# The order of a unit's half products in a hybrid decoder layer: the third factor's two halves around the seventh's

## The chip, the cores and the metric

The kernel runs on one core of one Trainium2 chip. The metric is the device time of one execution in microseconds. Three runs of the kernel before the change took 914.4, 915.17 and 915.88 us; the median is 915.17.

The core has a matrix engine (TensorE, PE in the profile, with the loading of its weights shown apart as PEld), a vector engine (VectorE, DVE), a scalar engine for activations and copies (ScalarE, ACT), a general engine (GpSimd, POOL) and SyncE (SP), which issues DMAs here. Matmuls write to PSUM, a memory of banks, from which ACT or DVE has to fetch the result before a bank can be used again.

## What is computed

The reference is one inference step of one decoder layer over 1024 prompt tokens and 8 decode tokens. All inputs to the branches come from one large projection of the normalised input; then a recurrent branch (RG-LRU) and a matrix memory (mLSTM, four heads of 256, chunks of 128 tokens) run, and a projection leads back:

```python
hn = rmsnorm(x, g_norm)
u = hn @ w_in                                  # 1024 x 1024 @ 1024 x 7176
xa, za, uq, uk, uv, uo, zb, ui, uf = jnp.split(u, SPLIT_IDX, axis=-1)
yA, hA, bufA = rglru_branch(xa, ...)           # conv, gates, linear scan
hB, C, n, m = mlstm_seq(q, k, v, ig, lf, C0, n0, m0)
yB = rmsnorm over a head of (sigmoid(uo) * hB), times g_mhead
merged = jnp.concatenate([yA * silu(za), yB * silu(zb)], axis=-1)
x = x + merged @ w_out
```

The first projection, `hn @ w_in`, is the part that the change concerns.

## The kernel before

Every matrix product is made exact to about float32 from a rounded high part and a low remainder of each operand: `mm3` (lines 64 to 68) issues high x high, high x low and low x high, always as three matmuls, and `split` (lines 70 to 74) makes the two parts with one ACT cast (line 72) and one DVE subtraction (line 73). In the profile nearly all matmuls therefore stand at L66, L67 and L68, and nearly all casts and subtractions at L72 and L73.

**Units and products.** The columns of `w_in` are worked off in 14 units of two blocks of 256 columns each (`UNITS`, line 44; the letters name what a block yields, v, x, y, q, k, o or z). Unit 0 is done while the input is read. A unit is a 2 x 2 block product by the scheme of Strassen and Winograd, with seven products instead of eight: P1, P2, P5, P6, P7, P3, P4 in this order (line 41). The input's seven combinations stand ready in `cb`; the weights' combinations are made unit by unit in `prep` (line 276), which also splits them into `wh` and `wl`. `prep` of P7 and P4 issues the loads of the next unit's weights on SP.

**Half products.** Each product is done in two halves, s = 0 and 1, here called pieces: 12 matmuls of 512 columns (24 of 256 in units of v and o). `product` (line 299) issues both one after the other. Each half has two PSUM accumulators, X (tag `kv`, two banks) and Y (tag `o`, three banks). P1, P6, P7 and P4 add up in the same X; P2 has a Y of its own, and P5 and P3 share the next one. After each piece `evac` (line 325) reads the partial sum:

- P1: ACT copies X to `s1` (L328). P2: DVE adds Y to `s1` (L331), output.
- P5: ACT copies Y to `s5` (L335).
- P6: ACT copies X to `s2` (L338).
- P7: DVE adds X to `s5` (L341), output.
- P3: DVE adds Y to `s2` (L345), output.
- P4: ACT copies X (L353), or applies tanh, output.

Outputs go to memory by `stq`, a DMA on POOL's queue (`emit_out`, line 362); for y and z a SiLU comes first (ACT L359, DVE L360). So P7 of a half must not start before the copy after P6 of that half has ended, and P4 not before the add after P7.

**Buffers.** `wh` and `wl` come from a pool of six (`NWS`), so three products are held; `LEAD = 2` calls `prep` two products ahead, and the split of a product can only begin when the product three before it has been used up. The staging tiles (`s1`, `s2`, `s5` and so on) come from a pool of seven.

**What runs beside it.** After each piece, `pop_bg` (line 711) issues one step, or two in the first and last units, of the background work: gates, the RG-LRU branch, the decode part, the first chunks of the mLSTM. In the last unit, `wo_due(q)` (line 1642), called after product q, appends steps that prepare the output projection: `w_step` splits blocks of `w_out` into buffers that held `cb` (those of P7 for one split, those of P3 for the next two), and `r_op` splits operands from a ring that SP fills, into tiles of the pool of six. After the units, `r_prod` multiplies the ring's operands, interleaved with the mLSTM's chunks.

The program is traced in this order; a scheduler then sorts each engine's instructions, by readiness in a model of the time and by the order of the program among those that are ready. Each engine then runs its list in order.

Of the kernel before, what the change touches and what calls it, by code (L numbers as in the profile page):

```python
# [17 lines left out]
P = 128  # L18
# [4 lines left out]
NH = 4  # L23
# [17 lines left out]
Q_P1, Q_P2, Q_P5, Q_P6, Q_P7, Q_P3, Q_P4 = range(7)  # L41
# [3 lines left out]
NWS, NSTG, LEAD = 6, 7, 2  # L45
# [6 lines left out]
def hymba_kernel(  # L52
# [11 lines left out]
    def mm3(out, ah, al, bh, bl, first, last):  # L64

        TE.matmul(out, ah, bh, start=first, stop=False, skip_group_check=True)  # L66
        TE.matmul(out, ah, bl, start=False, stop=False, skip_group_check=True)  # L67
        TE.matmul(out, al, bh, start=False, stop=last, skip_group_check=True)  # L68
# [13 lines left out]
    def ps(tag, shape):  # L82
        return psp.tile(shape, F32, tag=tag, name=f"ps_{tag}", bufs=NBUF.get(tag, 1))
# [17 lines left out]
    def sg(shape, name, dt=F32):  # L101

        return stg.tile(shape, dt, tag="stg", name=name)
# [116 lines left out]
    late = []  # L220
    lastt = []

    def run_late():
        now = late[:]
        late.clear()
        for f in now:
            f()
# [3 lines left out]
    units = [((c[0], int(c[1])), (c[2], int(c[3]))) for c in UNITS]  # L231
# [39 lines left out]
    wops = {}  # L271
# [24 lines left out]

    px = {}

    def product(u, q):

        kind = units[u][0][0]
        wh, wl = wops.pop((u, q))
        bh, bl = cb[q]
        first, last = q in (Q_P1, Q_P2, Q_P5), q in (Q_P2, Q_P3, Q_P4)
        for s in range(2):
            if q == Q_P1:
                px["X", s] = ps("kv", [P, 512])
            if q in (Q_P2, Q_P5):
                px["Y", s] = ps("o", [P, 512])
            X, Y = px["X", s], px.get(("Y", s))  # L310
            out = X if q in (Q_P1, Q_P6, Q_P7, Q_P4) else Y
            if kind in "vo":
                for i in range(2):
                    t = slice((2 * s + i) * P, (2 * s + i + 1) * P)
                    for k in range(4):
                        mm3(out[:, i * 256:(i + 1) * 256], bh[:, k, t], bl[:, k, t], wh[:, k, :], wl[:, k, :],
                            first and i == 0 and k == 0, last and i == 1 and k == 3)
            else:
                c = slice(s * P, (s + 1) * P)
                for k in range(4):  # L320
                    mm3(out, wh[:, k, c], wl[:, k, c], bh[:, k, :], bl[:, k, :], first and k == 0, last and k == 3)
            evac(u, q, s, X, Y)
            yield

    def evac(u, q, s, X, Y):
        if q == Q_P1:
            px["s1", s] = t = sg([P, 512], "s1")
            A.copy(t, X)  # L328
        elif q == Q_P2:
            t = px.pop(("s1", s))  # L330
            V.tensor_tensor(t, t, Y, op=ALU.add)  # L331
            emit_out(u, 0, 0, s, t)
        elif q == Q_P5:
            px["s5", s] = t = sg([P, 512], "s5")
            A.copy(t, Y)  # L335
        elif q == Q_P6:
            px["s2", s] = t = sg([P, 512], "s2")
            A.copy(t, X)  # L338
        elif q == Q_P7:
            t = px.pop(("s5", s))  # L340
            V.tensor_tensor(t, t, X, op=ALU.add)  # L341
            emit_out(u, 1, 1, s, t)
        elif q == Q_P3:
            t = px.pop(("s2", s))
            V.tensor_tensor(t, t, Y, op=ALU.add)  # L345
            emit_out(u, 0, 1, s, t)
        else:
            t = sg([P, 512], "c21")
            o = units[u][1][0] == "o"
            if o:  # L350
                A.activation(t, X, AF.Tanh, scale=0.5)
            else:
                A.copy(t, X)  # L353
            emit_out(u, 1, 0, s, t, o)
# [170 lines left out]
    kind, j = units[0][0]  # L525
# [183 lines left out]
    bg, rgq, dcq = deque(), deque(), deque()  # L709

    def pop_bg(n=1, rg=1, dc=1):
        run_late()
        for q, m in ((bg, n), (rgq, rg), (dcq, dc)):
            for _ in range(m):
                if q:
                    q.popleft()()
# [38 lines left out]
    def rg_unit(jj):  # L755

        rst["stored"] |= {2 * jj, 2 * jj + 1}
        for j in (2 * jj, 2 * jj + 1):
            for b in range(2):
                n = 2 * j + b  # L760
                h = rg_half(j, b)
                if n % 4 == 0:
                    rgq.append(lambda n=n: rg_load(n, True))
                rgq.extend(h[:-1])
                rgq.append((lambda j=j, f=h[-1]: (f(), rg_dec(j))) if b == 1 else h[-1])
        if jj == 3:
            rgq.extend([rg_final, lambda: None, rg_rows])
# [578 lines left out]
    def w_slot(a, b, n):  # L1346
        w_fetch(a, b, slot(n, f"wc{a}{b}", F32))
# [294 lines left out]
    def wo_due(q):  # L1642

        step = lambda *ns: bg.extend([lambda n=n: w_step(n) for n in ns])
        if q == 0:
            w_slot(0, 0, 0)
            w_slot(1, 0, 1)
        elif q == 1:
            w_slot(1, 1, 2)
        elif q == 2:  # L1650
            bg.append(lambda: dec_block(0))
            step("s3", Q_P1)
        elif q == 3:
# [12 lines left out]
    seq = [(u, q) for u in range(1, len(units)) for q in range(7)]  # L1666
    state = {"prep": 0, "m": False}

    def preps(n):
        while state["prep"] < min(n, len(seq)):  # L1670
            prep(*seq[state["prep"]])
            state["prep"] += 1
# [3 lines left out]
    last_u = len(units) - 1  # L1676
    unit_of = {p: u for u, pair in enumerate(units) for p in pair}
    done_h = [max(unit_of[k, h] for k in "qkv") for h in range(NH)]

    def m_start():  # L1680
        state["m"] = True
        bg.append(m_open1)
        for n in range(NH):
            bg.extend(m_first(n))

    preps(LEAD)
    part = 0
    for n, (u, q) in enumerate(seq):
        preps(n + 1 + LEAD)
        for _ in product(u, q):  # L1690
            pop_bg(2 if u == 1 or u == last_u else 1, 1, part % DEC[1 if u >= DEC[0] else 2] == 1)
            part += 1
        if u == last_u:
            wo_due(q)
        if q == 6:
            for kind, j in units[u]:
                if kind == "x":
                    rg_unit(j)
            for half in range(2):
                if u == max(unit_of["v", 2 * half], unit_of["v", 2 * half + 1], 1):  # L1700
                    bg.append(lambda half=half: dec_rows(half))
            for h in range(NH):
                if done_h[h] == u:
                    bg.append(lambda h=h: dcq.extend(decode_steps(h)))
            if u == last_u - 1:
                dgen = decode_outputs()

                def step():
                    next(dgen, None)
                    run_late()  # L1710
                state["out"] = [step] * 5 + [m_open2]
        if not state["m"] and u > max(done_h) and not (bg or rgq or dcq or late):
            m_start()
        if u == last_u and q == 0:
            if not state["m"]:
                while bg or rgq or dcq or late:
                    pop_bg()
                m_start()
            bg.extend(state["out"])
    while bg or late:  # L1720
        pop_bg()
    with tc.issue_after(lastt[0].ins):
# [6 lines left out]
    last = NCH - 1  # L1729
    N2 = 18  # L1730
    for n in range(4, N):
        c, h = n // 4, n % 4
# [92 lines left out]
```

## Time and profile before

| What | Value |
|---|---|
| Time of the runs | 914.4, 915.17, 915.88 us |
| The profiled execution | 913.23 us, its span 911.3 us |
| Units 1 to 13 on PE | from 72 us to 656 us |
| Busy between 0 and 72 us: PE, DVE, ACT | 68.5, 52.7, 46.3 us |
| Busy between 656 and 911.3 us: PE, DVE, ACT | 247.8, 209.3, 160.3 us |
| Moved by DMA | 167.76 MB, mean 184 GB/s |

A row of the profile names the engine, the line of the kernel, the operation, the tiles (written <- read) and either a duration or a count with the sum and the mean. A bracket at the end of a row gives the idle time of the engine before it and what ended that. Busy time counts an engine's own work, not its waiting for semaphores. The ends of matmuls are modelled, so the row of a matmul says more by its start than by its end.

### The profile page before, as it was taken

The page shows a single profiled execution, that of the slowest core. Times are in us where ns is not written, and L with a number is a line of the kernel's source. Part 1 is how long each engine was busy: PE and PEld are TensorE (multiplying, and loading weights), DVE is VectorE, ACT ScalarE, POOL GpSimd, SP SyncE. Part 2 cuts the span into 40 slices and gives each one's busy share as a digit, 9 for nine tenths or more (in the row PEclk, how much of TensorE's full clock was granted, in tenths as well). Part 3 has the DMA queues.
Part 4 walks back from the last instruction along what each step waited for, and adds up shares of the span by engine and source line. Part 5 has one row for each costly group of instructions (what it writes and reads, how often), then busy time and mean ns, then how long its engine had stood idle before and what let it go on. Part 6 is the DMA issues. An engine that isn't in the chain of part 4 may idle for free. (4 is left out here: it accounts for less than half of the span.)

```text
span 911.3 us, 16738 instructions
## 1 busy us (share of the span) xinstructions
PE 899.6 (99%) x5889; PEld 762.3 (84%) x5889; DVE 739.3 (81%) x1528; ACT 585.0 (64%) x1086; POOL 194.2 (21%) x322
## 2 busy tenths in 40 slices
PE   8999999999999999999999999999999999999996
PEld 6997778877788997887789999887788888888886
DVE  6974778979698978789889876679998879888973
ACT  7653446867567776576658775446786568566642
POOL 1111112122222232324332334010111111121120
PEclk9999999999999999999999999999999999999999
DMA  6412447465746566548665747345679888855531
GB/s 200 149 64 92 139 147 250 135 205 187 236 128 221 171 203 204 197 145 266 201 237 184 253 139 244 108 133 191 215 234 259 202 216 296 217 142 180 181 124 67
DMA packets 130493, 167.76 MB, mean 184 GB/s; under 512 B 17596, under 2 KB 98564, under 8 KB 130402
## 3 DMA queue, kind: packets, MB, share of 16 engines
q1 hardware_dynamic: 108790, 103.68, 37.4%
q0 software_dynamic: 21616, 63.02, 20.9%
q8 instruction: 46, 0.75, 0.3%
q14 instruction: 37, 0.30, 0.1%
q10 hardware_dynamic: 4, 0.00, 0.0%
HBM read 108.00 MB, written 62.92 MB: 188 GB/s over the span
## 5 line engine op out<-in xcount | busy, mean ns | idle before, releaser
L72 ACT CAST wh<-raw 128x1024 fp32r<-128x1024 f32 x91 | 95.4, 1049 | 79.5 <-DVE raw L280 21.0
L73 DVE TENSOR_TENSOR wl<-raw,wh 128x1024 fp32r<-128x1024 f32 x91 | 111.1, 1221 | 29.4 <-ACT wh L72 15.8
L66 PE MATMUL ps_kv<-cb_hi,wh 128*128 128x512 f32 x320 | 127.4, 398 | 0.0
L68 PE MATMUL ps_kv<-cb_hi,wl 128*128 128x512 f32 x320 | 125.5, 392 | 0.0
L67 PE MATMUL ps_kv<-cb_lo,wh 128*128 128x512 f32 x320 | 125.2, 391 | 0.0
L66 PE MATMUL ps_o<-cb_hi,wh 128*128 128x512 f32 x240 | 95.2, 397 | 0.0
L68 PE MATMUL ps_o<-cb_hi,wl 128*128 128x512 f32 x240 | 93.7, 391 | 0.0
L67 PE MATMUL ps_o<-cb_lo,wh 128*128 128x512 f32 x240 | 93.6, 390 | 0.0
L66 PEld LDWEIGHTS ps_kv<-cb_hi,wh 128*128 128x128 f32 x320 | 60.1, 188 | 15.9 <-issue 3.1
L68 PEld LDWEIGHTS ps_kv<-cb_hi,wl 128*128 128x128 f32 x320 | 60.1, 188 | 13.4 <-issue 0.6
L67 PEld LDWEIGHTS ps_kv<-cb_lo,wh 128*128 128x128 f32 x320 | 60.1, 188 | 12.7 <-issue 0.8
L66 PE MATMUL ps_kv<-wh,cb_hi 128*128 128x256 f32 x192 | 55.1, 287 | 0.0
L67 PE MATMUL ps_kv<-wl,cb_hi 128*128 128x256 f32 x192 | 54.4, 283 | 0.0
L68 PE MATMUL ps_kv<-wh,cb_lo 128*128 128x256 f32 x192 | 54.3, 283 | 0.0
L66 PEld LDWEIGHTS ps_o<-cb_hi,wh 128*128 128x128 f32 x240 | 45.1, 188 | 10.4 <-issue 0.8
L68 PEld LDWEIGHTS ps_o<-cb_hi,wl 128*128 128x128 f32 x240 | 45.0, 188 | 9.9
L66 PE MATMUL ps_o<-wo,mh 128*128 128x512 f32 (+1 forms) x136 | 53.0, 390 | 0.0
L67 PEld LDWEIGHTS ps_o<-cb_lo,wh 128*128 128x128 f32 x240 | 45.1, 188 | 8.9
L68 PE MATMUL ps_o<-wo,ml 128*128 128x512 f32 (+1 forms) x136 | 51.6, 380 | 0.0
L67 PE MATMUL ps_o<-wo,mh 128*128 128x512 f32 (+1 forms) x136 | 51.5, 379 | 0.0
L66 PE MATMUL ps_o<-wh,cb_hi 128*128 128x256 f32 x144 | 41.0, 284 | 0.0
L67 PE MATMUL ps_o<-wl,cb_hi 128*128 128x256 f32 x144 | 40.7, 283 | 0.0
(559 smaller groups left out, 2603.8 us busy)
## 6 DMA issues: line engine op xcount, KB each, us to landing
raw<-in_w_in_dram SPq DMA_DIRECT2D x55, 512.0 KB
Cb<-in_state_mlstm_C_dram SPq DMA_DIRECT2D x32, 256.0 KB
out_dram<-Cb POOLq DMA_DIRECT2D x32, 256.0 KB, 4.9
qk<-d_qk SPq DMA_DIRECT2D x32, 256.0 KB
ring<-d_ro SPq DMA_DIRECT2D x26, 256.0 KB
d_qk<-s POOLq DMA_DIRECT2D x24, 256.0 KB, 4.8
d_x<-s POOLq DMA_DIRECT2D x16, 256.0 KB, 2.8
zsr<-d_y SPq DMA_DIRECT2D x16, 256.0 KB
```

What stands on the lines that cost most here:

```text
L66: TE.matmul(out, ah, bh, start=first, stop=False, skip_group_check=True)
L67: TE.matmul(out, ah, bl, start=False, stop=False, skip_group_check=True)
L68: TE.matmul(out, al, bh, start=False, stop=last, skip_group_check=True)
L72: a = A.copy(hi, src)
L73: V.tensor_tensor(lo, src, hi.bitcast(F32), op=ALU.subtract)
```

## The change

`product` is no longer a generator of two halves but issues one half, given as `s`; the weights' tiles are dropped after the second half. The main loop goes over a list of 14 pieces. The first eight are as before. Then come P3's first half, P7's two halves, P3's second half, and P4's two. `PREP` gives the pieces before which `preps` is called: the sixth call, which starts the next unit's P1, comes before piece 11 instead of 10. `DUE` gives the pieces after which `wo_due` is called in the last unit: the call for index 4 comes after piece 10 (before: 9), that for 5 after piece 12 (before: 11).

```diff
-    def product(u, q):
+    def product(u, q, s):
 
         kind = units[u][0][0]
-        wh, wl = wops.pop((u, q))
+        wh, wl = wops.pop((u, q)) if s == 1 else wops[u, q]
...
-        for s in range(2):
...
-            evac(u, q, s, X, Y)
-            yield
...
+        evac(u, q, s, X, Y)
...
+    PIECES = [(q, s) for q in (Q_P1, Q_P2, Q_P5, Q_P6) for s in range(2)]
+    PIECES += [(Q_P3, 0), (Q_P7, 0), (Q_P7, 1), (Q_P3, 1), (Q_P4, 0), (Q_P4, 1)]
+    PREP = 0, 2, 4, 6, 8, 11, 12
+    DUE = 1, 3, 5, 7, 10, 12, 13
+
     preps(LEAD)
     part = 0
-    for n, (u, q) in enumerate(seq):
-        preps(n + 1 + LEAD)
-        for _ in product(u, q):
+    for u in range(1, len(units)):
+        for n, (q, s) in enumerate(PIECES):
+            if n in PREP:
+                preps(7 * (u - 1) + PREP.index(n) + 1 + LEAD)
+            product(u, q, s)
             pop_bg(2 if u == 1 or u == last_u else 1, 1, part % DEC[1 if u >= DEC[0] else 2] == 1)
             part += 1
-        if u == last_u:
-            wo_due(q)
...
+            if u == last_u and n in DUE:
+                wo_due(DUE.index(n))
```

The rest of the loop's body (the steps after a unit, the start of the mLSTM, the output steps of the decode part) is only indented and keyed to the piece's number; it comes after the same count of pieces as before.

More of the change, by code (lines that the diff above doesn't have):

```diff
@@ L297, in hymba_kernel @@
     px = {}
-    def product(u, q):
+    def product(u, q, s):
         kind = units[u][0][0]
-        wh, wl = wops.pop((u, q))
+        wh, wl = wops.pop((u, q)) if s == 1 else wops[u, q]
         bh, bl = cb[q]
         first, last = q in (Q_P1, Q_P2, Q_P5), q in (Q_P2, Q_P3, Q_P4)
-        for s in range(2):
[L306 to L319, printed above, removed]
-                for k in range(4):
-                    mm3(out, wh[:, k, c], wl[:, k, c], bh[:, k, :], bl[:, k, :], first and k == 0, last and k == 3)
-            evac(u, q, s, X, Y)
-            yield
+        if q == Q_P1:
+            px["X", s] = ps("kv", [P, 512])
+        if q in (Q_P2, Q_P5):
+            px["Y", s] = ps("o", [P, 512])
+        X, Y = px["X", s], px.get(("Y", s))
+        out = X if q in (Q_P1, Q_P6, Q_P7, Q_P4) else Y
+        if kind in "vo":
+            for i in range(2):
+                t = slice((2 * s + i) * P, (2 * s + i + 1) * P)
+                for k in range(4):
+                    mm3(out[:, i * 256:(i + 1) * 256], bh[:, k, t], bl[:, k, t], wh[:, k, :], wl[:, k, :],
+                        first and i == 0 and k == 0, last and i == 1 and k == 3)
+        else:
+            c = slice(s * P, (s + 1) * P)
+            for k in range(4):
+                mm3(out, wh[:, k, c], wl[:, k, c], bh[:, k, :], bl[:, k, :], first and k == 0, last and k == 3)
+        evac(u, q, s, X, Y)
     def evac(u, q, s, X, Y):
@@ L1691, in hymba_kernel @@
             pop_bg(2 if u == 1 or u == last_u else 1, 1, part % DEC[1 if u >= DEC[0] else 2] == 1)
             part += 1
-        if u == last_u:
-            wo_due(q)
[L1695 to L1717, printed above, removed]
-                m_start()
-            bg.extend(state["out"])
+            if u == last_u and n in DUE:
+                wo_due(DUE.index(n))
+            if n == 13:
+                for kind, j in units[u]:
+                    if kind == "x":
+                        rg_unit(j)
+                for half in range(2):
+                    if u == max(unit_of["v", 2 * half], unit_of["v", 2 * half + 1], 1):
+                        bg.append(lambda half=half: dec_rows(half))
+                for h in range(NH):
+                    if done_h[h] == u:
+                        bg.append(lambda h=h: dcq.extend(decode_steps(h)))
+                if u == last_u - 1:
+                    dgen = decode_outputs()
+                    def step():
+                        next(dgen, None)
+                        run_late()
+                    state["out"] = [step] * 5 + [m_open2]
@@ L1720, in hymba_kernel @@
+            if n % 2 and not state["m"] and u > max(done_h) and not (bg or rgq or dcq or late):
+                m_start()
+            if u == last_u and n == 1:
+                if not state["m"]:
+                    while bg or rgq or dcq or late:
+                        pop_bg()
+                    m_start()
+                bg.extend(state["out"])
     while bg or late:
```

## The prediction

> **What bounds the kernel now.** I read the head of the page first, then the busy time of each engine in six stretches, then what the matmul engine waited for.
>
> ```profile
> span 911.3 us, 16738 instructions
> PE 899.6 (99%) x5889; PEld 762.3 (84%) x5889; DVE 739.3 (81%) x1528; ACT 585.0 (64%) x1086; POOL 194.2 (21%) x322
> ...
> 72.00:292.00 220.00, 219.59 (x1324) 174.86 (x1321) 173.22 (x324) 136.38 (x201) 43.54 (x78) 1.00 0.54 174
> 292.00:470.00 178.00, 178.00 (x1229) 150.16 (x1221) 150.97 (x253) 120.64 (x172) 52.15 (x82) 1.00 0.62 202
> 470.00:611.00 141.00, 141.00 (x1168) 129.66 (x1168) 110.15 (x201) 91.07 (x148) 42.61 (x64) 1.00 0.57 186
> 611.00:656.00 45.00, 44.65 (x231) 33.54 (x220) 42.96 (x81) 30.26 (x45) 5.62 (x11) 1.00 0.58 194
> ...
> PE ps_s L1069 <- DVE dworkb L1067: 0.4, 1, 0.4
> PE ps_tr L257 <- DMA raw<-in_w_in_dram: 0.3, 1, 0.3
> ```
>
> The four stretches are those of the units whose pieces the change reorders (the columns are the stretch, its length, PE, PEld, DVE, ACT and POOL, the clock, the DMA share and GB/s). PE is busy for 219.59 + 178.00 + 141.00 + 44.65 = 583.24 of 584 us. So 0.76 us is idle, and the last two rows, the waits between 72 and 656 us, say for what: a small vector operation of the decode part and a weight load from memory. No evacuation of a half product is among them. The granted clock (the 1.00 behind the engines) is full. DVE is second, and only in the last 45 us is it nearly as full (42.96).
>
> A busy PE can hide stalls, since the ends of matmuls are modelled. So I look at starts, and at the load of weights beside them.
>
> ```profile
> 406.33 0.39 PE L68 MATMUL ps_kv<-cb_hi,wl 128*128 128x512 f32 x1
> 406.56 0.39 PE L66 MATMUL ps_kv<-cb_hi,wh 128*128 128x512 f32 x1
> ...
> L66 PEld LDWEIGHTS ps_kv<-cb_hi,wh 128*128 128x128 f32 x320 | 60.1, 188 | 15.9 <-issue 3.1 <-ACT xh L813 0.4 <-ACT c L353 0.2
> ```
>
> Start to start is 0.23 us, and the row at 406.56 is the first matmul of P7's first half, right behind P6: the border of two pieces costs no more than any other step. A piece of twelve such matmuls is 2.7 us. The Trainium skill, in "Perfetto Trace Analysis", section "Identifying the Most-Contended Engine", calls matmul busy time a poor measure of headroom and the busy share of weight loads a good one; by it the 84% of PEld would leave a sixth of the time open. Here the trace speaks against that reading: a load of 188 ns in every step of 230 ns is 82%, with the matmuls back to back.
>
> **The change part by part.** No instruction is added or removed, so all that can move the time is a wait, new or gone. Times are those of the profiled execution, 913.23 us (span 911.3 and 1.9 around it); the median of the three runs is 915.17, and I add my sum to the median.
>
> *P3's first half between P6 and P7.* P7 adds to the bank that P6's copy (L338) reads. Today one piece lies between a P6 half and the P7 half on the same bank; after, two. The tightest case of the 26 is unit 8, second half:
>
> ```profile
> 408.19 0.59 ACT L338 COPY s<-ps_kv 128x512 f32<-128x512 f32 x1
> ...
> 409.28 0.39 PE L66 MATMUL ps_kv<-cb_hi,wh 128*128 128x512 f32 x1
> ```
>
> The copy ends at 408.78 and P7 begins at 409.28: 0.5 us to spare without the change. So the wait that the change makes roomier is not there, and this part gains 0.
>
> *P7 closer to P4.* P4 writes the same bank as P7, after the vector engine's add (L341). Three pieces lie between today, two after. The latest add:
>
> ```profile
> 147.92 0.39 PE L68 MATMUL ps_kv<-cb_hi,wl 128*128 128x512 f32 x1
> ...
> 151.67 0.68 DVE L341 TENSOR_TENSOR s<-s,ps_kv 128x512 f32<-128x512 f32 x1
> ```
>
> P7's last matmul began at 147.92 and the next piece at 148.15; the add ended at 152.35, 4.2 us later. Two pieces give 5.4 us. So 1.2 us is left in the worst case: 0.
>
> *P3 needed two pieces sooner.* P3's weights are cast and split while P6 runs, at the same place as before, but are now used right after P6 and not four half products later. The split ends with the vector operation at L73. P3 would begin where P7's first half begins now:
>
> ```profile
> 98.00 1.22 DVE L73 TENSOR_TENSOR wl<-raw,wh 128x1024 fp32r<-128x1024 f32 x1 [4.20 <-PE ps_kv L67]
> 98.06 0.69 PE L616 MATMUL ps_s<-idF,par 49*128 49x49 f32 x8
> 98.69 0.50 PE L66 MATMUL ps_kv<-cb_hi,wh 128*128 128x512 f32 x1
> ...
> 139.83 1.23 DVE L73 TENSOR_TENSOR wl<-raw,wh 128x1024 fp32r<-128x1024 f32 x1
> 142.66 0.39 PE L66 MATMUL ps_kv<-cb_hi,wh 128*128 128x512 f32 x1
> ...
> 315.86 1.22 DVE L73 TENSOR_TENSOR wl<-raw,wh 128x1024 fp32r<-128x1024 f32 x1
> 317.70 0.28 PE L66 MATMUL ps_kv<-wh,cb_hi 128*128 128x256 f32 x1
> ...
> 447.52 1.23 DVE L73 TENSOR_TENSOR wl<-raw,wh 128x1024 fp32r<-128x1024 f32 x1
> 450.00 0.39 PE L66 MATMUL ps_kv<-cb_hi,wh 128*128 128x512 f32 x1
> ...
> 631.65 1.20 DVE L73 TENSOR_TENSOR wl<-raw,wh 128x1024 fp32r<-128x1024 f32 x1
> 637.86 0.39 PE L66 MATMUL ps_kv<-cb_hi,wh 128*128 128x512 f32 x1
> ```
>
> Split's end against P7's start: 99.22 against 98.69 in unit 1 (late by 0.5), then 141.06 / 142.66 (1.6 to spare, unit 2), 317.08 / 317.70 (0.6, unit 6), 448.75 / 450.00 (1.2, unit 9), and 632.85 / 637.86 (5.0, unit 13, the roomiest); the other eight lie between 1.6 and 5.0. In unit 1 the first two matmuls of a triple need only the high part, so two steps of 0.23 us pass first: 0.5 - 0.46 is a stall of 0.1 us. The row at 98.00 also says why it is late: it got its buffer only when P6's last reader was done. Bounds: 0 (other matmuls fill it, as the transposes at 98.06 do now) to 1.3 us (nothing does, so the whole split shows). I take 0.1. Nothing queues behind the wait but the next pieces.
>
> *The next unit's P1 is split one piece later*, since its buffer is P7's. Tightest case, unit 3: the split begun at 152.26 against P1's first matmul.
>
> ```profile
> 152.26 1.22 DVE L73 TENSOR_TENSOR wl<-raw,wh 128x1024 fp32r<-128x1024 f32 x1
> ...
> 161.00 0.50 PE L66 MATMUL ps_kv<-cb_hi,wh 128*128 128x512 f32 x1
> ```
>
> From 153.48 to 161.00 there are 7.5 us; 2.7 less leaves 4.8: 0. P3's and P7's stores on POOL change places, with POOL 21% busy and their staging buffers freed by completion; no SP load moves but those of the tail.
>
> *The last unit's background steps.* Those that follow P7 and P3 (weight splits, ring loads) come one piece later in the program, and P7's buffers come free one piece later.
>
> ```profile
> 645.38 0.62 ACT L72 CAST ro<-ring 128x512 fp32r<-128x512 f32 x1 [1.12 <-PE ps_kv L67]
> ...
> 653.62 0.69 DVE L73 TENSOR_TENSOR ro<-ring,ro 128x512 fp32r<-128x512 f32 x1
> ...
> 656.30 0.39 PE L66 MATMUL ps_o<-wr0h,ro 128*128 128x512 f32 x1
> ```
>
> The cast of the first ring operand waited for a buffer of P7. A piece later it ends at 648.7, still 4.9 us ahead of the vector operation that completes it, so that one need not move. It ends at 654.3, 2.0 us ahead of its matmul. Bounds: 0, and 0.7 us at this matmul if the vector operation slips by a whole piece as well. DVE has the same work and takes P3's add early for P7's late one: I take 0.
>
> Sum: 0.1 us, 915.3.
>
> **Rivals.** *The tail slips by a whole piece (slower).* DVE is full there, and this chain follows:
>
> ```profile
> 667.55 2.28 DVE wr5l L73 x2
> ...
> 670.22 3.89 DMA ring<-d_ro
> ...
> 674.65 0.48 ACT hh L1247
> 675.18 0.66 PE ps_qp L1298 x4
> ```
>
> From the split of the last weights over a ring load to a PE that already waits, each microsecond that DVE loses arrives in full. If DVE idles for the piece that the splits wait, that is 2.7 us: 917.9. It decides once DVE's loss passes 1.8 us. For it: the chain has no slack. Against it: DVE's work is sorted by readiness there, and the ring cast above shows 4.9 us of room. *P3's splits run late in many units (slower).* If the later P1 split of one unit pushes the vector work of the next by d, stalls are 0.1 + d in unit 1 and d less the margins 0.6, 1.2 and 1.6. At d = 2 us that is 2.1 + 1.4 + 0.8 + 0.4 = 4.7: 919.9. It passes 0.2% at about d = 1.2. Against it: in each unit all vector work up to P6 is as before.
>
> *Hidden stalls go (faster).* All idle time of the units, 0.76, and the slow matmuls:
>
> ```profile
> L66 PE MATMUL ps_kv<-cb_hi,wh x320: 387/389/504, 72.5 to 655.6; 128*128 128x512 f32 x160
> ...
> L66 PE MATMUL ps_kv<-cb_hi,wh 128*128 128x512 f32 x320 | 127.4, 398 | 0.0
> L68 PE MATMUL ps_kv<-cb_hi,wl 128*128 128x512 f32 x320 | 125.5, 392 | 0.0
> L67 PE MATMUL ps_kv<-cb_lo,wh 128*128 128x512 f32 x320 | 125.2, 391 | 0.0
> ```
>
> Means of 398, 392 and 391 over a median of 389 ns are 14 ns x 320 = 4.5 us in the four products on this bank, 1.1 for P7's share. With 0.76 that is 1.9: 913.3. It needs every one of them to hang on P6's copy, and the 0.5 us above speaks against. The rule of the Trainium skill on weight loads, taken at its word, would be this case. *The change doesn't do what it says:* where P3's split is late, P7 may still be issued first, since the schedule already interleaves by readiness in the tail. Then the order is partly the old one: 915.2.
>
> **How the numbers follow.** Two runs can be told apart from about 0.2%, or 1.8 us. Forecast, 0.76: 915.3. Order partly unchanged, 0.04: 915.2. Together 0.80 within 0.2%. Tail, 0.07: 917.9, and late splits, 0.06: 919.9; slower 0.13. Hidden stalls, 0.07: 913.3; faster 0.07. The range leaves out these three, 0.20 in all: from 913.6, the lowest run of before (914.4) less all idle time of the units (0.76), to 917.2, the highest run (915.88) and the upper bound of P3's stall in unit 1 (1.3).
>
> **What would show it.** Right: PE idle between 72 and 656 us stays under 1.5 us, the ACT copy L338 ends some 3 us ahead of P7, and unit 1 shows P3's third matmul up to 0.5 us late. Wrong: PE waits on DVE L73 at the start of P3 in units 6, 9 or 2 (late splits); the wait at L1298 near 675 us grows past 2 us, or a new one stands at the first ring matmul (tail); or the spacing at P7 falls and the span with it (hidden stalls).

## The result and the profile after

The changed kernel took 920.4 us (median of six runs, 919.19 to 922.85) against 915.67 us (914.4 to 915.88, six runs) of the kernel before: ratio 1.0051, 95% interval 1.004 to 1.0061. It is slower by half a per cent. The forecast was 915.3 us, with a range from 913.6 to 917.2 us.

The profiled execution took 920.19 us. First the head of its page:

```profile
span 918.4 us, 16730 instructions
PE 901.3 (98%) x5889; PEld 763.0 (83%) x5889; DVE 739.7 (81%) x1528; ACT 585.1 (64%) x1086; POOL 194.6 (21%) x322
```

The counts of PE, DVE, ACT and POOL are those of before, and so are the busy times of DVE, ACT and POOL, within 0.4 us. The work is the same. What grew is mostly waiting; PE's busy time is 1.7 us longer with the same count. The same four stretches as in the prediction (stretch, length, PE, PEld, DVE, ACT, POOL, clock, DMA share, GB/s):

```profile
72.00:292.00 220.00, 218.98 (x1293) 174.09 (x1290) 172.51 (x325) 135.34 (x201) 43.64 (x78) 1.00 0.54 173
292.00:470.00 178.00, 177.64 (x1201) 149.57 (x1204) 146.78 (x244) 118.89 (x170) 51.01 (x79) 1.00 0.61 200
470.00:611.00 141.00, 136.78 (x1145) 125.67 (x1146) 111.00 (x200) 90.49 (x146) 42.80 (x64) 1.00 0.56 183
611.00:656.00 45.00, 44.65 (x276) 33.77 (x275) 41.32 (x84) 26.65 (x41) 5.64 (x11) 1.00 0.55 184
```

PE idles 1.02 + 0.36 + 4.22 + 0.35 = 5.95 us, where before it idled 0.76 us: 5.2 us of the 7.1 us by which the span grew (918.4 against 911.3). The two medians lie only 4.7 us apart, since the profiled execution of before was 2.4 us under its median. The other 1.9 us are not idle time of PE in the units, and nothing here explains them. Most of the idle time, 4.2 us, lies in the third stretch, where before PE had none. What PE waited for between 72 and 656 us (total, times, longest):

```profile
PE ps_kv L66 <- ACT c L351: 2.7, 2, 1.9
PE ps_s L924 <- DVE OC L911: 0.9, 1, 0.9
PE ps_o L66 <- DVE s L329: 0.8, 2, 0.5
PE ps_s L818 <- DVE xh L812: 0.4, 1, 0.4
PE ps_s L1067 <- DVE dworkb L1065: 0.4, 1, 0.4
PE ps_s L655 <- DVE gx L625: 0.3, 1, 0.3
PE ps_kv L66 <- ACT c L349: 0.3, 1, 0.3
```

The lines behind `evac`'s beginning stand two lower than before: L351 is L353 of before, the copy after P4; L329 is L331, the add after P2. The largest wait is a first matmul of P1 in unit 10, which may not write its bank before ACT has copied unit 9's P4 from it. The prediction never looked at that hand-off.

The timeline of **before** around it, first ACT, then DVE and PE:

```profile
456.62 1.05 ACT L72 CAST wh<-raw 128x1024 fp32r<-128x1024 f32 x1 [1.10 <-PE ps_kv L67]
...
462.08 0.72 ACT L988 ACTIVATE Cb<-Cb,dGI 128x512 f32<-128x512 f32 x1 [2.16 <-DMA Cb<-in_state_mlstm_C_dram]
462.71 0.80 ACT L834 ACTIVATE rg<-rg,sp4n 128x512 f32<-128x512 f32 x1
...
467.13 0.59 ACT L353 COPY c<-ps_kv 128x512 f32<-128x512 f32 x1
470.80 0.62 ACT L813 CAST xh<-xc 64x512 fp32r<-64x512 f32 x1 [3.08 <-DVE na L847]
471.84 0.62 ACT L813 CAST xl<-xc 64x512 fp32r<-64x512 f32 x1 [0.42 <-DVE rm L865]
472.48 0.59 ACT L353 COPY c<-ps_kv 128x512 f32<-128x512 f32 x1
...
469.55 1.22 DVE L847 TENSOR_TENSOR_SCAN na<-rg,ig 128x512 f32<-128x512 f32 x1
...
467.80 0.39 PE L68 MATMUL ps_kv<-cb_hi,wl 128*128 128x512 f32 x1
...
473.61 0.39 PE L66 MATMUL ps_kv<-wh,cb_hi 128*128 128x256 f32 x1
```

And **after**:

```profile
466.09 0.72 ACT L986 ACTIVATE Cb<-Cb,dGI 128x512 f32<-128x512 f32 x1 [4.76 <-DMA Cb<-in_state_mlstm_C_dram]
466.72 0.80 ACT L832 ACTIVATE rg<-rg,sp4n 128x512 f32<-128x512 f32 x1
467.43 1.04 ACT L72 CAST wh<-raw 128x1024 fp32r<-128x1024 f32 x1
...
471.99 0.59 ACT L351 COPY c<-ps_kv 128x512 f32<-128x512 f32 x1
475.88 0.62 ACT L811 CAST xh<-xc 64x512 fp32r<-64x512 f32 x1 [3.31 <-DVE na L845]
476.92 0.61 ACT L811 CAST xl<-xc 64x512 fp32r<-64x512 f32 x1 [0.42 <-DVE rm L863]
477.56 0.59 ACT L351 COPY c<-ps_kv 128x512 f32<-128x512 f32 x1
...
462.50 0.68 DVE L339 TENSOR_TENSOR s<-s,ps_kv 128x512 f32<-128x512 f32 x1
...
468.50 1.23 DVE L73 TENSOR_TENSOR wl<-raw,wh 128x1024 fp32r<-128x1024 f32 x1 [0.25 <-ACT wh L72]
...
474.63 1.22 DVE L845 TENSOR_TENSOR_SCAN na<-rg,ig 128x512 f32<-128x512 f32 x1
...
472.63 0.38 PE L66 MATMUL ps_kv<-wh,cb_hi 128*128 128x256 f32 x1 [0.77 <-ACT c L351]
...
478.20 0.38 PE L66 MATMUL ps_kv<-wh,cb_hi 128*128 128x256 f32 x1 [1.90 <-ACT c L351]
```

Read them as one chain through two queues. A load of decode state (`Cb`) ends; ACT, which has stood still for it, scales it (L988, after: L986), then computes an exponential for the RG-LRU branch (L834 / L832). Several vector operations further on, DVE does the branch's scan (L847 / L845). The next casts of that branch on ACT (L813 / L811) write into tiles that the scan and the product behind it (L865 / L863) still read, so they wait for both. Only behind them comes the second copy of P4, though P4 had long ended: in before its last matmul began at 467.80, 4.7 us ahead of that copy. Before, that copy ended at 473.07 and P1's second half began at 473.61: **0.54 us to spare**.

The cast of the next unit's P1 is the row that changed its place. Before, it ran at 456.62, released by one of P7's last matmuls and ahead of the whole chain. After, P7 ends a piece later, DVE's add on it starts at 462.50, and by then ACT already stands at the scale. The cast (467.43) and its subtraction (468.50, 1.23 us on DVE) now run between the exponential and the scan. The Trainium skill, in "Perfetto Trace Analysis", section "Tensor Engine Instruction (MATMUL, LD_WEIGHTS)", says that the queues of ACT and DVE are strictly first in, first out; the 4.76 us that ACT idles with that cast behind the scale agree.

So two things make the copy late. From the scale to the second copy it took 472.48 - 462.08 = 10.40 us before and 477.56 - 466.09 = 11.47 us after: 1.07 us more. And the scale itself began 4.01 us later. The rest of this text asks which part of the change is behind that, and whether it is the whole loss.

### The profile page after: what moved, and what is told of

Same layout as the page of the kernel before. It is cut to its first block, busy times and chain, and to the rows that moved or that the text cites. A ratio compares the mean times of both kernels' runs of the same rounds, so it can differ in the third digit from the quotient of the medians.

```text
span 918.4 us, 16730 instructions
## 1 busy us (share of the span) xinstructions
PE 901.3 (98%) x5889; PEld 763.0 (83%) x5889; DVE 739.7 (81%) x1528; ACT 585.1 (64%) x1086; POOL 194.6 (21%) x322
## 5 line engine op out<-in xcount | busy, mean ns | idle before, releaser
L73 DVE TENSOR_TENSOR wl<-raw,wh 128x1024 fp32r<-128x1024 f32 x91 | 110.9, 1219 | 34.3 <-ACT wh L72 19.2
L67 PE MATMUL ps_kv<-cb_lo,wh 128*128 128x512 f32 x320 | 125.2, 391 | 0.0
L67 PE MATMUL ps_o<-cb_lo,wh 128*128 128x512 f32 x240 | 93.6, 390 | 0.0
L67 PEld LDWEIGHTS ps_kv<-cb_lo,wh 128*128 128x128 f32 x320 | 60.1, 188 | 12.7 <-issue 0.8
L67 PE MATMUL ps_kv<-wl,cb_hi 128*128 128x256 f32 x192 | 54.4, 283 | 0.0
L67 PEld LDWEIGHTS ps_o<-cb_lo,wh 128*128 128x128 f32 x240 | 45.1, 188 | 8.8
L67 PE MATMUL ps_o<-wo,mh 128*128 128x512 f32 (+1 forms) x136 | 51.5, 379 | 0.0
L67 PE MATMUL ps_o<-wl,cb_hi 128*128 128x256 f32 x144 | 40.7, 283 | 0.0
```

The source lines that it names most:

```text
L73: V.tensor_tensor(lo, src, hi.bitcast(F32), op=ALU.subtract)
```

## The experiments

Each time is a median, and each ratio is to the kernel before in the same series of runs. There the kernel before had medians of 914.41, 914.1, 914.59 and 914.2 us.

### First series: what the traces suggested

Three ideas were open: the later split of the next unit's P1, P3 between P6 and P7, and the steps of the last unit. A fourth kernel moved the scale.

**The split alone, in the old order.** Only the call that issues the next unit's P1 split comes one piece later:

```diff
-        preps(n + 1 + LEAD)
+        if q != Q_P3:
+            preps(n + 1 + LEAD)
         for s, _ in enumerate(product(u, q)):
...
+            if q == Q_P3 and s == 0:
+                preps(n + 1 + LEAD)
```

> The order of pieces of the kernel before, with one thing of the change: the split of the next unit's P1 is issued one piece later (before P3's second half instead of its first). Theory A (the later split of the next unit's P1 shifts the scalar engine's queue, and P4's copies behind it come too late for the next unit's P1): 919 to 922 us, over 3 us of PE idle between 72 and 656 us, most of it at the start of unit 10 behind the copy L353. Theory B (P3 between P6 and P7 does it: its weights are needed two pieces sooner, and the adds change places): 915 to 916.5 us, under 1.2 us idle there. Theory C (the last unit's steps come later): 915 to 916.5 us as well.

Measured: 913.84 us, ratio 0.9997 (0.9987 to 1.0007). By the time alone the split would be cleared. The timeline of ACT in this run says why it must not be:

```profile
456.29 1.05 ACT L72 CAST wh<-raw 128x1024 fp32r<-128x1024 f32 x1 [1.10 <-PE ps_kv L67]
```

The cast runs at 456.29, as in before (456.62). The scheduler sorts by readiness, and the buffers were free at the old time. The edit moved a line of the program and not the instruction, so this run tells nothing of a late split.

**P7 first.** The changed kernel with P7_0, P3_0, P7_1, P3_1, so that P3 no longer follows P6 at once; P7 still ends a piece later than before.

```diff
-    PIECES += [(Q_P3, 0), (Q_P7, 0), (Q_P7, 1), (Q_P3, 1), (Q_P4, 0), (Q_P4, 1)]
+    PIECES += [(Q_P7, 0), (Q_P3, 0), (Q_P7, 1), (Q_P3, 1), (Q_P4, 0), (Q_P4, 1)]
```

> The changed kernel with P7's first half ahead of P3's first half (P7, P3, P7, P3): P7 follows P6 at once as in the kernel before and P3 is needed one piece later than in the changed one, but P7 still ends a piece later, so the late split of the next unit's P1 stays. Theory A: 919 to 922 us with the stall at the start of unit 10. Theory B: back towards 915 to 917 us.

Measured: 919.33 us, ratio 1.0056 (1.0036 to 1.0075). The loss stays, and PE's largest wait is the same one:

```profile
PE ps_kv L66 <- ACT c L351: 2.3, 2, 1.9
```

So P3's place right behind P6 is not the cause. What this order shares with the changed one is P7's end.

**The last unit's steps.** The changed kernel with one of the two later steps of `wo_due` back at its old piece:

```diff
-    DUE = 1, 3, 5, 7, 10, 12, 13
+    DUE = 1, 3, 5, 7, 10, 11, 13
```

> The changed kernel, with the last unit's step for index 5 issued after piece 11 again instead of 12. Theories A and B: unchanged, 919.5 to 921.5 us, since the time was lost before the last unit. Theory C: 917 to 919 us.

Measured: 918.67 us, ratio 1.0047 (1.0026 to 1.0068): the loss stays.

**The scale on VectorE.** The changed kernel with `V.tensor_scalar` in place of `A.mul` for `Cb` (L986), so that ACT no longer stands still for the load.

> The changed kernel with the scaling of the decode state (L986, which waits for a load) done by the vector engine instead of the scalar engine. Theory A, with the scalar engine's queue held up behind that wait: the stall of 2.8 us at the start of unit 10 goes, 916.5 to 918.5 us, as long as the 32 added vector operations of some 0.4 us find room. Theory B: 920 to 922 us.

Measured: 921.96 us, ratio 1.0084 (1.0064 to 1.0105). In its timeline DVE takes over the wait:

```profile
465.48 0.48 DVE L986 TENSOR_SCALAR Cb<-Cb,dGI 128x512 f32<-128x512 f32 x1 [6.86 <-DMA Cb<-in_state_mlstm_C_dram]
```

DVE now idles 6.86 us with its part of the same chain behind it. Moving the wait to another queue that the chain also passes mended nothing.

### Second series: when P7's buffers come free

If not the line of the program but the freeing of P7's buffers sets the split's time, that must be moved by itself.

**Freed early, in the new order.** P7's second half reads P3's weights, so P7's buffers come free at the old piece. That half product then computes something else.

```diff
         wh, wl = wops.pop((u, q)) if s == 1 else wops[u, q]
+        if q == Q_P7 and s == 1:
+            wh, wl = wops[u, Q_P3]
...
-    PREP = 0, 2, 4, 6, 8, 11, 12
+    PREP = 0, 2, 4, 6, 8, 10, 12
```

> The changed kernel, but the seventh product's second half reads the third product's weights, and the next unit's first split is issued ahead of it again. So the seventh's two weight buffers come free one piece sooner, as before the change; order, evacuations and stores stay as changed. What is computed by that half product is not the reference's. Theory A2 (the loss is the next unit's first split, which starts when the seventh's last half frees its buffers, and then stands inside the chain on ScalarE and VectorE that the fourth product's copies wait behind): back at the time before, 914 to 916 us, ratio 0.999 to 1.0015, and TensorE idle under 1.5 us from 72 to 656 us. Rival B2 (the loss is the order itself: later adds and stores of the seventh, earlier need and add of the third): 918.5 to 920.5 us, ratio 1.004 to 1.006.

Measured: 913.74 us, ratio 0.9995 (0.9983 to 1.0007). The whole loss is gone, to within this interval, with the new order, its evacuations, its stores and both later steps of `wo_due` unchanged. The chain has its old length (lines stand two higher than in the changed kernel):

```profile
463.27 0.73 ACT L988 ACTIVATE Cb<-Cb,dGI 128x512 f32<-128x512 f32 x1 [3.65 <-DMA d_qk<-s]
...
473.67 0.58 ACT L353 COPY c<-ps_kv 128x512 f32<-128x512 f32 x1
```

**Held one piece longer, in the old order.** Built on the first experiment: the last three matmuls of P3's first half (s == 0) read P7's weights, kept in `px["hold"]`, and so compute something else.

```diff
+        if q == Q_P7:
+            px["hold"] = wh, wl
...
                 for k in range(4):
+                    if q == Q_P3 and s == 0 and k == 3:
+                        wh, wl = px["hold"]
                     mm3(out, wh[:, k, c], wl[:, k, c], bh[:, k, :], bl[:, k, :], first and k == 0, last and k == 3)
```

(In units of v and o the same stands at i == 1 and k == 3, and the second half takes its own weights again.)

> The kernel before, in its old order, but the last three matmuls of the third product's first half read the seventh product's weights, so that those buffers come free one piece later, and the next unit's first split is issued behind that piece. Those matmuls compute something else. Theory A2: slow as the changed kernel, 918.5 to 921 us, ratio 1.004 to 1.007, with TensorE waiting for the fourth product's copies (L353) at the start of unit 10. Rival B2: 914 to 915.5 us, ratio within 0.001 of 1.

Measured: 918.66 us, ratio 1.004 (1.0027 to 1.0053). Holding two buffers for one more piece makes the old order about as slow as the new one. The two runs together show the cause, to within their intervals: **the time at which P7's buffers come free, and nothing else of the order.** The profiled execution was this kernel's fastest run, 915.75 us (the other four took 918.49 to 918.79), so its sum of waits is small. Its chain has the same form, though (lines stand eight higher here):

```profile
462.35 0.72 ACT L996 ACTIVATE Cb<-Cb,dGI 128x512 f32<-128x512 f32 x1 [2.75 <-DMA Cb<-in_state_mlstm_C_dram]
...
463.69 1.03 ACT L72 CAST wh<-raw 128x1024 fp32r<-128x1024 f32 x1
...
473.82 0.59 ACT L361 COPY c<-ps_kv 128x512 f32<-128x512 f32 x1
```

From scale to second copy: 473.82 - 462.35 = 11.47 us, to the hundredth that of the changed kernel. Set beside the runs whose cast comes early:

| Kernel | P7's buffers free | Scale begins | Second copy of P4 begins | Distance |
|---|---|---|---|---|
| before | early | 462.08 | 472.48 | 10.40 |
| split alone | early | 462.85 | 473.24 | 10.39 |
| freed early | early | 463.27 | 473.67 | 10.40 |
| after | late | 466.09 | 477.56 | 11.47 |
| P7 first | late | 464.51 | 475.98 | 11.47 |
| last unit's steps | late | 466.68 | 478.15 | 11.47 |
| held one piece | late | 462.35 | 473.82 | 11.47 |

The late split costs this chain 1.07 us in each of these four, twice the 0.54 us that the hand-off had to spare. The start of the scale, on the other hand, scatters: it hangs on the end of a transfer. In five of the seven traces the profile names the load of `Cb`; in "freed early" and "P7 first" it names a store (`d_qk<-s`).

The wait for P4's copy follows both. In these executions it is 0 in before, 0.5 us with the split alone, 0.9 freed early and 0.7 held, though the held chain is the longer one; it is 2.3 to 2.7 us in the other three, whose scale begins late as well. So the rows show how the split reaches the hand-off, but not that the 1.07 us by themselves make the whole loss.

**The scale on GpSimd,** in the changed kernel: `G.tensor_scalar` for `A.mul`.

> The changed kernel, with the decode state's scale (L986) on GpSimd, so that its wait for the load of that state stands neither in ScalarE's queue nor in VectorE's. Theory A3 (two things must meet: the split one piece later, and the wait for the state's load at the head of ScalarE's queue): unit 10's wait of 2.8 us goes, and most of unit 11's with it, 915 to 917 us, ratio 1.0005 to 1.003. Rival A4 (the split's own 1.2 us inside VectorE's chain is enough): half of unit 10's wait stays, 917 to 919 us. Rival B2: 919 to 920.5 us.

Measured: 930.45 us, ratio 1.0172 (1.0156 to 1.0189), far off every expectation. Two rows of its groups and waits:

```profile
L986 POOL TENSOR_SCALAR Cb<-Cb,dGI 128x512 f32<-128x512 f32 x32 | 54.7, 1712 | 30.6 <-DMA Cb<-in_state_mlstm_C_dram 29.4 <-PE ps_o L68 0.6 <-PE ps_o L257 0.2
```

```profile
DVE Cb L988 <- POOL Cb L986: 14.9, 8, 7.1
```

One scale takes 1712 ns there, and VectorE's next step on the state waits for it, 14.9 us in all. The wait has come back to DVE's queue, through the result. I had only thought of the queue that the scale left, and not of the instruction that needs its result.

**Held two pieces longer,** the same edit at s == 1.

> As the run before it but one, with the seventh's weights read by the last three matmuls of the third product's second half, so that the buffers come free two pieces later. Theory A2: slower than with one piece, 921 to 927 us, ratio 1.007 to 1.014, since the split then ends after the time that its product wants it in some units. Rival B2: 914 to 915.5 us.

Measured: 916.23 us, ratio 1.0025 (1.0015 to 1.0034): slower than before, but far under the 921 to 927 us that were expected. Its interval overlaps that of one piece (1.0027 to 1.0053), so it is not shown to be less; it is not more. More delay is not more loss. In its trace the cast runs at 468.77, behind ACT's work for the scan, so that the distance from scale to second copy is 474.91 - 463.79 = 11.12 us. This fits that what counts is which instructions the split lands among.

### Third series: moving the decode's steps

If the loss is a meeting of the split with the decode step's wait, moving the decode's token steps should move it. In units 1 to 9 they come after every third piece; two kernels of each order shift them by one.

```diff
-            pop_bg(2 if u == 1 or u == last_u else 1, 1, part % DEC[1 if u >= DEC[0] else 2] == 1)
+            pop_bg(2 if u == 1 or u == last_u else 1, 1, part % DEC[1 if u >= DEC[0] else 2] == (1 if u >= DEC[0] else 0))
```

(With 2 in place of the last 0 for one piece later.)

> The changed kernel, with the decode's token steps of units 1 to 9 at pieces whose number leaves 0 on division by 3 instead of 1, that is, one piece sooner. Theory A3 (the loss is a meeting of two things in unit 9: the split one piece later, and the wait for the state's load in the decode step): the meeting is moved, and the distance to the kernel before with the same token steps (third kernel of this job) falls under 3 us. Rival A5 (a later split costs as much wherever the token steps stand): the distance stays between 4 and 6 us. In numbers for this one: 914 to 918 us by A3, 918.5 to 921 us by A5.

> As the first kernel of this job, with the token steps one piece later than in the changed kernel. A3: the distance to the kernel before with the same token steps (fourth kernel) falls under 3 us, 914 to 918 us. A5: it stays between 4 and 6 us, 918.5 to 921 us.

> The kernel before with the token steps of units 1 to 9 one piece sooner: the control of the first kernel of this job. Both theories: 913.5 to 916 us, since TensorE has only 0.76 us idle in these units to win and its hand-offs 0.5 us or more to lose.

> The kernel before with the token steps of units 1 to 9 one piece later: the control of the second kernel of this job. Both theories: 913.5 to 916 us.

| Token steps | Old order | New order | Distance |
|---|---|---|---|
| one piece sooner | 919.68, ratio 1.005 (1.0032 to 1.0068) | 918.92, ratio 1.0042 (1.0027 to 1.0057) | -0.8 us |
| one piece later | 914.94, ratio 1.0005 (0.9996 to 1.0015) | 918.28, ratio 1.0042 (1.0027 to 1.0056) | 3.3 us |

The first control failed: the old order with the token steps sooner is as slow as the new one. Its PE waits:

```profile
PE ps_kv L66 <- ACT s L338: 2.6, 2, 1.6
PE ps_kv L66 <- ACT c L353: 1.6, 1, 1.6
PE ps_o L66 <- DVE s L331: 1.4, 1, 1.4
```

These are evacuations again, and the largest is the copy after P6 (L338). Here, then, the hand-off that the change was to relieve does make PE wait, and in the new order with the same token steps no wait for that copy is left; other waits (1.9 us for P2's add, 1.3 for P4's copy) stand there in its place. From the timeline of ACT in the same kernel:

```profile
462.24 0.72 ACT L988 ACTIVATE Cb<-Cb,dGI 128x512 f32<-128x512 f32 x1 [7.17 <-DMA Cb<-in_state_mlstm_C_dram]
...
478.07 0.59 ACT L353 COPY c<-ps_kv 128x512 f32<-128x512 f32 x1
```

ACT idles 7.17 us for the state's load, with the exponential and all that follows it behind the scale, and P4's second copy comes at 478.07, 5.6 us later than in before. So the old order owes its time to the place of its token steps too; with these one piece sooner, the change costs nothing more. With the steps later, the old order keeps its time (the scale runs at 456.25, clear of the chain), and the new one still loses 3.3 us: its largest wait is then the one for the tile `OC` (1.2 us), and P4's copy is down to 0.7 us. Neither theory is borne out as written: by one row the distance falls under 3 us, by the other it does not.

### Fourth series: the two parts of the delay

**No wait for the state's load.** The load goes to a tile that nobody reads, and the scale reads a constant; the decode's states are then not the reference's. In both orders:

```diff
-            ds_["C", i] = t = fpr["p"].tile([P, 2, 256], F32, tag="Cb", name="Cb", bufs=4)
-            ld(t, st_C[0, b, h].rearrange("(kb p) v -> p kb v", p=P))
+            ds_["C", i] = t = fpr["p"].tile([P, 2, 256], F32, tag="Cb", name="Cb", bufs=3)
+            cin = fpr["p"].tile([P, 2, 256], F32, tag="cin", name="cin", bufs=2)
+            ld(cin, st_C[0, b, h].rearrange("(kb p) v -> p kb v", p=P))
...
-                A.mul(C, C, dGI[:, b, h:h + 1])
+                A.mul(C.rearrange("p k (a c) -> p (k a) c", c=P), idF.unsqueeze(1).to_broadcast([P, 4, P]), dGI[:, b, h:h + 1])
```

> The changed kernel; the decode state is still loaded, into a tile that nobody reads, and the scale on ScalarE reads a constant in its place, so that nothing waits for that load. The decode's states are not the reference's. Theory A3 (both together, the wait for the load the larger part): unit 10's wait for the fourth product's copies falls from 2.8 us to under 1 us, 914.5 to 917 us. Rival A4 (the subtraction inside VectorE's chain is enough): 917.5 to 920 us. Rival A6 (the load's wait is the whole): 913.5 to 915 us, as the control.

> The kernel before with the same edit, the control of the run before it. All theories: 913 to 915.5 us, since TensorE waits for almost nothing there.

Measured: 924.76 us, ratio 1.011 (1.0092 to 1.0129), in the new order, and 921.01 us, ratio 1.0075 (1.0059 to 1.0091), in the old. The control is slow by itself, so the times cannot be set beside before. Against its own control the new order is still 3.75 us slower, which speaks against the load's wait as the larger part. The windows show that the edit made a loss of its own elsewhere. The control:

```profile
72.00:292.00 220.00, 214.40 (x1252) 169.52 (x1245) 165.98 (x312) 130.25 (x190) 40.29 (x73) 0.99 0.58 188
...
470.00:611.00 141.00, 141.00 (x1166) 129.30 (x1164) 111.43 (x200) 91.50 (x145) 42.71 (x64) 1.00 0.54 174
```

PE idles 5.6 us in the first stretch, where before it idled 0.41. The new order with the same edit:

```profile
470.00:611.00 141.00, 139.79 (x1157) 128.13 (x1157) 109.99 (x196) 90.45 (x141) 43.59 (x66) 1.00 0.55 176
```

In the third stretch, where the changed kernel idles 4.22 us, it idles 1.21 us, and no wait for P4's copy is among it. That speaks for the load's wait as a part of the loss. The two readings point different ways, and the pieces meet other steps here, so how large the part is stays open.

**No subtraction in the next unit's P1 split.** The changed kernel; P1's matmuls read P2's low parts in its place, and compute something else. The cast stays.

```diff
+        if q == Q_P1 and u > 1:
+            wl = wops[u, Q_P2][1]
...
-        split(hi, lo, blk(u, *src[q]))
+        if q == Q_P1 and u > 1:
+            A.copy(hi, blk(u, *src[q]))
+        else:
+            split(hi, lo, blk(u, *src[q]))
```

> The changed kernel without the subtraction of the first product's split (from the second pass's unit on); its matmuls read the second product's low parts in its place, which computes something else. The cast stays where it is. A3: unit 10's wait falls by about the 1.1 us that the subtraction adds to the chain, 917 to 919.5 us. A4: 914 to 916 us. A6: 919 to 921 us.

Measured: 916.77 us (914.19 to 918.92), ratio 1.0028 (1.0018 to 1.0038). Of the changed kernel's ratio, 1.0051, not quite half goes with this one VectorE operation per unit. The old order was not run with this edit, so how much of that is only less work on VectorE (twelve operations of 1.2 us) isn't known. The third stretch, in the fastest run, which the profile shows:

```profile
470.00:611.00 141.00, 140.88 (x1162) 129.30 (x1155) 106.38 (x197) 91.22 (x148) 43.36 (x65) 1.00 0.58 187
```

PE idles 0.12 us there; no wait for P4's copy is left in this execution. But the chain is hardly shorter (lines stand five higher than in the changed kernel):

```profile
461.83 0.72 ACT L991 ACTIVATE Cb<-Cb,dGI 128x512 f32<-128x512 f32 x1 [1.80 <-DMA Cb<-in_state_mlstm_C_dram]
...
473.13 0.59 ACT L356 COPY c<-ps_kv 128x512 f32<-128x512 f32 x1
```

From scale to second copy it takes 473.13 - 461.83 = 11.30 us, 0.17 us less than the 11.47 us with the subtraction. On DVE the subtraction of P2's split now runs early in its place, at 465.19, ahead of an operation of the branch that it follows in the changed kernel. So the expectation that the subtraction is what lengthens the chain does not hold; the wait is gone here because the scale begins early, at 461.83. A median of 2.6 us over before, 916.77 against 914.2, stays.

**Both edits.**

> The changed kernel with both edits: no wait for the state's load, no subtraction in the first product's split. A3: 913.5 to 915.5 us, the time before. If something beside these two costs as well, it stays above 916 us.

Measured: 921.4 us, ratio 1.0074 (1.0054 to 1.0094). The first edit's own loss is in it, so the time cannot be set beside before; no theory had foreseen that. Within the scatter it is the time of the old order with the first edit (921.01 us); the new order with the first edit alone was 3.75 us slower than that. But the old order with both edits was not run, so this does not show the subtraction to be the loss.

## Why the prediction was wrong

- **PE is saturated in the units, so only a new or a vanished wait can move the time.** Right. PE's idle time there grew from 0.76 to 5.95 us, and the span by 7.1.
- **P3 between P6 and P7 gains nothing, since P6's copy is done in time.** Right. P6's copies now end further ahead of P7; in the case that was tightest, unit 8's second half, P7 begins at 413.79 and the copy ended at 409.99 + 0.59 = 410.58, 3.2 us ahead, and nothing is won by it:

```profile
409.99 0.59 ACT L336 COPY s<-ps_kv 128x512 f32<-128x512 f32 x1
...
413.79 0.39 PE L66 MATMUL ps_kv<-cb_hi,wh 128*128 128x512 f32 x1
```

- **P7 closer to P4: 0.** No wait of P4 for P7's add (L339) stands in PE's waits after.
- **P3 needed two pieces sooner: 0.1 us.** No wait on L73 stands there either. In unit 1, P3's third matmul began at 99.98, 0.70 us behind the second (99.28) in place of 0.23. So it came about 0.5 us late, as forecast, and two matmuls of P7 (99.51 and 99.74) filled the gap, which is the lower bound of that term. With P7 first the loss stays, so this part cost nothing that can be seen. The "four half products later" in the prediction's text is a slip: between P6 and P3 lay two, as its heading says, and no number hangs on it.
- **"The next unit's P1 is split one piece later ... 0."** This is the step that failed. I asked whether the split would be late for its own product, found 4.8 us left in the tightest unit, and stopped. For P1 that was right: its weights were ready 2.9 us ahead even in unit 10. But the split is also 1 us of ACT and 1.2 us of DVE, in queues that others share, and it was moved to another place in them. I priced its lateness and not its company. Who now stands behind it is a chain that ends in P4's copy, a hand-off with 0.54 us to spare, which my list of margins (P6 to P7, P7 to P4, P3's weights) did not contain. In place of the 0, holding the buffers one piece longer in the old order cost 4.6 us (918.66 against 914.1), and freeing them early in the new order took the loss away (913.74). So this step carries the loss, as far as the intervals can tell.
- **The rival of late P3 splits** had half of it: it supposed that "the later P1 split of one unit pushes the vector work of the next", gave it 919.9 us, and let it hurt P3's weights. The push was there, but what it delayed were the evacuations at the border to the next unit, not that unit's P3. Its price was near by accident.
- **The rival of the tail** (917.9) fell: with one step back at its old piece the loss stays, and with both late and P7's buffers freed early there is none. After the units PE's waits are 0.6 us at L1296 and 0.3 at L67, against 0.4 at L1298 before.
- **Hidden stalls, and order partly unchanged:** neither came. The order did change, but for the two matmuls of P7 in unit 1. PEld's share of 84% became 83% in a longer span, and no run found room in the rest.

What stays open: how the loss divides. The 1.07 us in the chain are shown in seven traces, and taking the subtraction out gave back not quite half of the loss, but hardly by way of this chain. Whether the state's load ends later for the new order's sake could not be separated either: in the new order's three traces with a late release the scale begins at 464.51 to 466.68, with an early release at 462.08 to 463.27. But PE was already later in the former, the held run has 462.35, and the edit that was to remove the wait made a new loss. Nor was it tried to keep the new order and free P7's buffers early with the right weights; a fourth pair of weight buffers doesn't fit into the memory as the kernel divides it. None of the runs beat the kernel before by more than its scatter; with 0.76 us of idle time in the units there was little to win.

## What to carry to other kernels

When an operation moves, price it in the queues that it moves through: who stands behind it there, and which hand-off waits for them last, with the spare time of every hand-off to the bound engine listed and not only those that the change names. An order of uses is also an order of frees: what the next tenant of a buffer does then moves too, and the line of the program that issues it may not matter at all. And a control belongs to each edit that shifts work, since a kernel in which PE hardly ever waits can owe that to one lucky spacing; the run without the subtraction has none, and can't be read for that reason.

## What was unexpected in the hardware's numbers

- A scale of 128 x 512 float32 took 1712 ns on GpSimd, and 0.48 us on VectorE in the same place (the row at 465.48). The Trainium skill, in "GPSIMD Engine Reference", section "4.1 Engine selection", calls an elementwise operation with one input "roughly line-rate" on GpSimd. Here it took 3.5 times as long there as on VectorE, and the measurement decides.
- The same chain of eleven microseconds over two engines repeated to 0.01 us in three and four kernels (10.39 to 10.40 and 11.47), while the scale at its head, which waits for a transfer, began anywhere from 462.08 to 466.68. That suggests the scatter of this kernel's time comes from its transfers and not from its engines, but each kernel has one trace only, and the kernels differ, so it is not shown.
